# Keeping the split weights of the first attention's projections in DRAM for the second half of the tokens

## The chip, the core and the metric

The kernel runs on one core of a Trainium2 chip. The metric is the time of one execution on the device, in microseconds; three executions of the kernel before took 3351.19 to 3359.43 us, with a median of 3356.41 us. The engines are named as in the profile: PE is TensorE's matmul, PEld its weight load, DVE is VectorE, ACT is ScalarE, POOL is GpSimd, and SP is SyncE, which issues the transfers.

## What is computed

Two blocks are applied to 2048 tokens of 1024 features. The first block is a short convolution mixer and then a stick-breaking attention with 8 heads of 64. The change concerns the four projections of that attention:

```python
kv = _rmsnorm(x, norm_kv) @ w_kv            # w_kv: 1024 x 1024
k, v = jnp.split(kv, 2, axis=-1)
...
h = _rmsnorm(x, norm_b[j])
q, g = jnp.split(h @ w_in_b[j], 2, axis=-1) # w_in_b: 1024 x 1024
...
o = _stick_breaking_attention(q, k, v)
x = x + (o * jax.nn.silu(g)) @ w_out_b[j]
```

The second block has a gated pooling mixer and an attention over the 256 best keys of an indexer (`w_in`, `w_out`). Everything is float32.

## The kernel before

**Precision.** A float32 product is made of three matmuls in the type `fp32r`. Each operand is split into a rounded part `hi` and a remainder `lo`, and `lin` (L112 to L122) adds `hi*hi`, `hi*lo` and `lo*hi` (L119, L120, L121) over the blocks of 128 features. One call of `lin` makes 128 outputs for 512 tokens, with 24 matmuls for 1024 features.

**Stages.** Tokens are handled in two halves of 1024. `phase_a(h)` is the convolution mixer, `phase_b(h)` makes k, v, q and the gate of the attention, `phase_c(h)` is the attention itself, `phase_d` its output projection and the next norm, `phase_e` and `phase_e2` the second block's projections, `phase_f` its attention and `phase_g` the output. `phase_b` first normalises the tokens (`norm_x`, L313 to L320: load from `x1d`, multiply on DVE at L319, round on ACT at L81, subtract on DVE at L82), and then runs through 16 blocks of 128 columns: eight of `w_kv` (four k, four v) and eight of `w_in_b` (four q, four gate). For each block it calls `load_w` once and `lin` twice (512 tokens each), and stores k, q (`hi` and `lo` each), v or the gate to DRAM. `phase_c` loads them again: z is two matmuls (L533, L534), ACT's sigmoid follows (L536), DVE's scan (L546) and multiply (L547), the transposes on PE (L553), ACT's copy (L555) and the matmul with v (L561).

**Weights.** `load_w` makes two tiles for a block of 1024 features, one for each four blocks of features. A tile is loaded raw into one of two buffers (`raw`, shown as `fixed`), for `w_kv` and `w_in_b` multiplied by the norm's gain on DVE (L103), rounded on ACT into the `hi` half of one of four slots (`weights`, shown as `fixedr`; L104), and the remainder is put into the `lo` half by DVE (L105). A slot holds 512 KB, a raw tile 256 KB. With `keep` the slot is also stored to DRAM (L107 to L109, `kept_<name>_<column>_<block>`), and a later call with the same name, column and block loads the slot from there at L95 and skips the rest. Before the change that is so for `w_out`, `w_out_b`, `w_in` and `w_pool`; `w_in_a` and `w_out_a` are called with `keep=False`; `w_kv` and `w_in_b` are left out by name at L106. All transfers are issued by SP (`dma`, L75 to L77), in order, so all show line L77.

**Order.** The phases are generators, merged by weights; `ahead` raises the priority of one of them, and a planner then lays out the instructions of each engine by data dependences, priorities and its own estimate of times. The calls around the change are:

```python
run(self.phase_b(0, xa))                                                    # L1340
merge((self.phase_b(1, xb), 167), (self.ahead(self.phase_c(0), 2000), 95))  # L1342
merge((self.ahead(self.phase_c(1), 2000), 260), (de, 300))                  # L1344
```

So `phase_b(0)` runs alone (about 905 to 1100 us in the profile), `phase_b(1)` runs beside the attention of the first half (about 1100 to 1480 us), and after that the attention of the second half runs beside `phase_d(0)` and `phase_e(0)`.

Of the kernel before, what the change touches and what calls it, by code (L numbers as in the profile page):

```python
# [68 lines left out]
class Build:  # L69
# [14 lines left out]
    def load_w(self, name, nk, c0, m=P, gain=None, after=None, keep=True, own=None):  # L84

        nc = self.nc
        hi, lo = [], []
        for k0 in range(0, nk, 4):
            t = self.turn("weights", 4) if own is None else own
            hi += [t[:, 0, k] for k in range(4)]  # L90
            lo += [t[:, 1, k] for k in range(4)]
            if (name, c0, k0) in self.kept:
                if after is not None:
                    nc.gpsimd.tensor_copy(t[:, :, 0, 0:1], after.unsqueeze(2).to_broadcast([P, 2, 1]))
                self.dma(t, self.kept[name, c0, k0])  # L95
                continue
            raw = self.turn("raw", 2)
            if m < P:
                nc.gpsimd.memset(raw, 0.0)
            self.dma(raw[:, :, :m], self.I[name][k0 * P : (k0 + 4) * P, c0 : c0 + m].rearrange("(k p) m -> p k m", p=P))  # L100
            if gain is not None:
                g = self.vec[:, gain + k0 : gain + k0 + 4]
                nc.vector.tensor_tensor(raw, raw, g.unsqueeze(2).to_broadcast([P, 4, P]), ALU.mult)  # L103
            nc.scalar.activation(t[:, 0], raw, AF.Copy)  # L104
            nc.vector.tensor_tensor(t[:, 1], raw, t[:, 0].bitcast(F32), ALU.subtract)  # L105
            if keep and name not in ("w_kv", "w_in_b"):  # L106
                d = self.dr.tile([P, 2, 4, P], F32R, name=f"kept_{name}_{c0}_{k0}")  # L107
                self.dma(d, t)
                self.kept[name, c0, k0] = d  # L109
        return hi, lo  # L110
# [1369 lines left out]
```

## Time and profile before

| | before |
|---|---|
| median of 3 executions | 3356.41 us |
| lowest, highest | 3351.19, 3359.43 us |
| the profiled execution | 3360.51 us |
| its span, first to last instruction | 3358.8 us |
| mean granted clock of TensorE | 0.977 |
| PE, DVE, ACT busy | 96%, 67%, 45% of the span |

Busy shares are means over stages with different limits, so the stretches of the two calls of `phase_b` are read one by one. A busy PE is not PE at its peak, since the ends of matmuls are modelled and overlap; the starts of matmuls and the busy time of the weight loads say how fast it really goes. The granted clock stands as a share of full speed, between the level 1.2 GHz (0.5) and 2.4 GHz (1.00).

### The profile page before, as it was taken

The page shows a single profiled execution, that of the slowest core. Times are in us where ns is not written, and L with a number is a line of the kernel's source. Part 1 is how long each engine was busy: PE and PEld are TensorE (multiplying, and loading weights), DVE is VectorE, ACT ScalarE, POOL GpSimd, SP SyncE. Part 2 cuts the span into 40 slices and gives each one's busy share as a digit, 9 for nine tenths or more (in the row PEclk, how much of TensorE's full clock was granted, in tenths as well). Part 3 has the DMA queues.
Part 4 walks back from the last instruction along what each step waited for, and adds up shares of the span by engine and source line. Part 5 has one row for each costly group of instructions (what it writes and reads, how often), then busy time and mean ns, then how long its engine had stood idle before and what let it go on. Part 6 is the DMA issues. An engine that isn't in the chain of part 4 may idle for free.

```text
span 3358.8 us, 49679 instructions
## 1 busy us (share of the span) xinstructions
PE 3212.6 (96%) x18050; PEld 2546.6 (76%) x18050; DVE 2249.0 (67%) x4516; ACT 1501.3 (45%) x2794; POOL 470.9 (14%) x584
## 2 busy tenths in 40 slices
PE   8999999999999999998899999889999999999997
PEld 7888888788878778776678887667877777666775
DVE  5344534545253878788888788798946878799741
ACT  4111421111232544465555555565365555776571
POOL 0000010000100000033312112331110143103002
PEclk9999999999999999997999999889999999999998
DMA  3111452424454455474456544554553265115115
GB/s 105 48 48 47 138 169 88 132 85 138 129 179 154 143 153 160 127 245 131 117 157 182 171 141 158 168 168 135 172 164 105 84 214 171 47 39 172 46 30 180
DMA packets 371683, 439.77 MB, mean 131 GB/s; under 512 B 25696, under 2 KB 271968, under 8 KB 371424
## 3 DMA queue, kind: packets, MB, share of 16 engines
q1 hardware_dynamic: 371424, 436.44, 42.1%
q8 instruction: 147, 2.41, 0.3%
q14 instruction: 112, 0.92, 0.1%
HBM read 309.46 MB, written 125.30 MB: 129 GB/s over the span
## 4 chain that ended last, share of the span: by engine, by line
PE 78%; DVE 13%; ACT 3%; issue 3%; DMA 2%; POOL 0%; SPq 0%; ACTq 0%; DVEq 0%; POOLq 0%
PE lin L119 11%; PE lin L120 10%; PE lin L121 10%; PE z L119 4%; PE z L120 4%; PE z L121 4%; PE o L561 4%; PE o L1221 3%; PE tp L553 3%; PE tp L1213 3%; PE tp L120 3%; PE tp L119 3%; PE tp L121 3%; DVE crf L546 2%; PE z L533 2%
## 5 line engine op out<-in xcount | busy, mean ns | idle before, releaser
L119 PE MATMUL lin<-act,fixedr 128*128 128x512 f32 x1488 | 597.4, 402 | 15.0 <-DVE x1r L597 7.9
L120 PE MATMUL lin<-act,fixedr 128*128 128x512 f32 x1488 | 595.2, 400 | 9.5 <-DVE act L618 7.2
L121 PE MATMUL lin<-act,fixedr 128*128 128x512 f32 x1488 | 592.2, 398 | 0.0
L104 ACT ACTIVATE fixedr<-fixed 128x512 fp32r<-128x512 f32 x294 | 185.9, 634 | 726.1 <-PE lin L120 263.2
L546 DVE TENSOR_TENSOR_SCAN crf<-crf 128x512 f32<-128x512 f32 (+3 forms) x320 | 354.6, 1116 | 74.0 <-ACT crf L543 71.4
L119 PEld LDWEIGHTS lin<-act,fixedr 128*128 128x128 f32 x1488 | 284.0, 191 | 80.3 <-DVE x1r L597 9.8
L120 PEld LDWEIGHTS lin<-act,fixedr 128*128 128x128 f32 x1488 | 283.8, 191 | 74.3 <-DVE act L618 10.0
L105 DVE TENSOR_TENSOR fixedr<-fixed,fixedr 128x512 fp32r<-128x512 f32 x294 | 203.5, 693 | 197.7 <-ACT fixedr L104 186.2
L121 PEld LDWEIGHTS lin<-act,fixedr 128*128 128x128 f32 x1488 | 283.7, 191 | 61.0 <-issue 0.2
L1162 DVE CUSTOM_DVE_ANT_0 fe<-z,masks 128x512 f32<-128x512 f32 (+3 forms) x320 | 188.3, 605 | 105.0 <-PE tp L1213 53.3
L119 PE MATMUL z<-act,fixedr 128*128 128x512 f32 x584 | 231.7, 397 | 9.3 <-ACT fixedr L104 9.3
L536 ACT ACTIVATE crf<-z 128x512 f32<-128x512 f32 (+3 forms) x320 | 175.3, 549 | 144.6 <-PE tp L553 109.8
L555 ACT COPY crf<-tp 128x512 f32<-128x512 f32 (+3 forms) x320 | 164.9, 532 | 156.0 <-PE tp L553 135.8
L120 PE MATMUL z<-act,fixedr 128*128 128x512 f32 x584 | 231.0, 396 | 0.0
L121 PE MATMUL z<-act,fixedr 128*128 128x512 f32 x584 | 230.9, 396 | 0.0
L549 POOL TENSOR_TENSOR crf<-crf 128x1 f32<-128x1 f32 x192 | 93.2, 487 | 928.8 <-ACT crf L536 732.5
L1176 ACT ACTIVATE fe<-fe,fixed 128x1024 f32<-128x1024 f32 (+7 forms) x192 | 189.7, 992 | 71.6 <-DVE fixed L1173 70.8
L1215 ACT COPY ff<-tp 128x512 f32<-128x512 f32 (+3 forms) x320 | 161.2, 523 | 127.2 <-PE o L1221 65.7
L883 DVE SCALAR_TENSOR_TENSOR sc<-ff,fixed,sc 128x512 f32<-128x512 f32 (+3 forms) x266 | 180.8, 702 | 52.3 <-ACT ff L876 50.5
L547 DVE TENSOR_TENSOR crf<-crf 128x511 f32<-128x511 f32 (+3 forms) x320 | 199.8, 630 | 10.7 <-PE lin L121 0.5
L1213 PE MATMUL tp<-fixed,fe 128*128 128x128 f32 x1088 | 181.8, 282 | 21.0 <-ACT fe L1176 16.4
L876 ACT ACTIVATE ff<-z 128x512 f32<-128x512 f32 (+3 forms) x304 | 158.2, 547 | 92.2 <-PE z L874 73.1
(346 smaller groups left out, 6541.5 us busy)
## 6 DMA issues: line engine op xcount, KB each, us to landing
fixed<-in_w_in_a_dram SPq DMA_DIRECT2D x128, 256.0 KB, 2.7
fixedr<-kept_w_out SPq DMA_DIRECT2D x64, 512.0 KB, 4.8
kept_w_in<-fixedr SPq DMA_DIRECT2D x46, 512.0 KB, 4.1
fixedr<-kept_w_in SPq DMA_DIRECT2D x46, 512.0 KB, 4.0
crr<-kst SPq DMA_DIRECT2D x80, 256.0 KB, 5.4
crr<-qst SPq DMA_DIRECT2D x64, 256.0 KB, 5.4
fixed<-x2d SPq DMA_DIRECT2D x64, 256.0 KB, 3.8
ffr<-q2s SPq DMA_DIRECT2D x128, 128.0 KB, 2.9
```

The source lines that it names most:

```text
L104: nc.scalar.activation(t[:, 0], raw, AF.Copy)
L105: nc.vector.tensor_tensor(t[:, 1], raw, t[:, 0].bitcast(F32), ALU.subtract)
L119: self.nc.tensor.matmul(ps[:, :n], whi[k], a, start=k == 0, stop=False)
L120: self.nc.tensor.matmul(ps[:, :n], whi[k], b, start=False, stop=False)
L121: self.nc.tensor.matmul(ps[:, :n], wlo[k], a, start=False, stop=k == nk - 1)
L536: nc.scalar.activation(s[:, :W], z[:, :W], AF.Sigmoid)
L546: nc.vector.tensor_tensor_scan(er, er, er, left, ALU.mult, ALU.min)
L547: nc.vector.tensor_tensor(s[:, : W - 1], s[:, : W - 1], e[:, 1:W], ALU.mult)
L883: nc.vector.scalar_tensor_tensor(sc[:, c0 : c0 + m], r[:, :m], w, sc[:, c0 : c0 + m], ALU.mult, ALU.add)
L1162: nc.vector.tensor_tensor_reduce(row[c0 // HT][:, c0 % HT : c0 % HT + m], z[:, :m], mb[:, c0 : c0 + m], 1.0, NEG, ALU.subtract, ALU.max, m ...
L1176: nc.scalar.activation(x, x, AF.Exp, bias=nbs, scale=sc, accum_out=den[:, u, hd : hd + 1])
L1213: nc.tensor.transpose(tp[:, j * P : (j + 1) * P], pe[a][k0 // HT][:, k0 % HT : k0 % HT + P], self.ident)
```

## The change

The exclusion of `w_kv` and `w_in_b` at L106 is dropped:

```diff
-            if keep and name not in ("w_kv", "w_in_b"):
+            if keep:
                 d = self.dr.tile([P, 2, 4, P], F32R, name=f"kept_{name}_{c0}_{k0}")
                 self.dma(d, t)
                 self.kept[name, c0, k0] = d
```

`phase_b(0)` now stores each of its 32 split tiles (16 blocks of columns, two tiles each) to DRAM, with the gain already in them. `phase_b(1)` loads them from there at L95 into the weight slots, without the raw buffer, the multiply of L103, the rounding of L104 and the subtraction of L105.

## Rows read from the trace of the kernel before

**Rows 1.** Head of the page: span, busy time and share by engine.

```profile
span 3358.8 us, 49679 instructions
PE 3212.6 (96%) x18050; PEld 2546.6 (76%) x18050; DVE 2249.0 (67%) x4516; ACT 1501.3 (45%) x2794; POOL 470.9 (14%) x584
```

**Rows 2.** Busy time by stretch: from:to, length, engines in order, clock, DMA, GB/s.

```profile
core 0: us, PE busy (x) PEld busy (x) DVE busy (x) ACT busy (x) POOL busy (x), PEclk, DMA share, GB/s
960.00:1100.00 140.00, 140.00 (x637) 115.82 (x635) 53.17 (x81) 31.67 (x55) 0.00 (x0) 1.00 0.58 175
1100.00:1480.00 380.00, 372.00 (x2297) 294.40 (x2297) 310.10 (x537) 186.63 (x388) 29.56 (x52) 0.99 0.54 161
1120.00:1220.00 100.00, 94.12 (x562) 73.16 (x560) 87.82 (x164) 49.93 (x107) 5.31 (x11) 0.97 0.56 165
1240.00:1340.00 100.00, 99.90 (x652) 80.60 (x651) 82.73 (x155) 43.31 (x97) 4.65 (x10) 1.00 0.56 147
1340.00:1480.00 140.00, 137.99 (x852) 108.47 (x851) 105.48 (x158) 73.91 (x142) 17.89 (x28) 1.00 0.55 180
```

**Rows 3.** PE's waits, 1100 to 1480 us: releaser, us in total, times, longest.

```profile
PE lin L120 <- DVE act L82: 2.3, 1, 2.3
PE z L533 <- DMA crr<-qst: 1.8, 1, 1.8
```

**Rows 4.** Groups by line, 1110 to 1400 us: busy, mean ns, idle before, releaser.

```profile
L104 ACT ACTIVATE fixedr<-fixed 128x512 fp32r<-128x512 f32 x28 | 17.7, 635 | 33.0 <-PE lin L120 30.0 <-DVE fixed L103 3.0
...
L103 DVE TENSOR_TENSOR fixed<-fixed 128x512 f32<-128x512 f32 x29 | 20.0, 690 | 36.2 <-DMA fixed<-in_w_in_b_dram 22.3 <-DMA fixed<-in_w_kv_dram 13.8
L105 DVE TENSOR_TENSOR fixedr<-fixed,fixedr 128x512 fp32r<-128x512 f32 x28 | 19.0, 678 | 0.0
```

**Rows 5.** DVE in order of time, phase_b(1)'s norm: first and last of nine.

```profile
1126.14 0.67 DVE L105 TENSOR_TENSOR fixedr<-fixed,fixedr 128x512 fp32r<-128x512 f32 x1
...
1180.80 0.67 DVE L105 TENSOR_TENSOR fixedr<-fixed,fixedr 128x512 fp32r<-128x512 f32 x1
```

**Rows 6.** Stores: KB each, median us to landing; then landing of kept_w_in's 46 loads.

```profile
kept_w_in<-fixedr SPq DMA_DIRECT2D x45, 512.0 KB, 4.1
...
DMA to landing us min/median/max: 3.1/4.0/8.6
```

**Rows 7.** phase_b(0): ACT and DVE in order of time; DVE's waits, 905 to 960 us.

```profile
1057.61 0.63 ACT L104 ACTIVATE fixedr<-fixed 128x512 fp32r<-128x512 f32 x1 [0.66 <-PE z L120]
1068.49 0.63 ACT L104 ACTIVATE fixedr<-fixed 128x512 fp32r<-128x512 f32 x1 [1.90 <-PE lin L120]
...
1058.89 0.68 DVE L105 TENSOR_TENSOR fixedr<-fixed,fixedr 128x512 fp32r<-128x512 f32 x1
...
1062.20 0.69 DVE L103 TENSOR_TENSOR fixed<-fixed 128x512 f32<-128x512 f32 x1 [0.51 <-DMA fixed<-in_w_in_b_dram]
...
DVE fixed L319 <- DMA fixed<-x1d: 2.7, 6, 1.0
```

**Rows 8.** SP's waits, 1100 to 1480 us; then 2170 to 2620 us.

```profile
SPq L77 <- DVE fixedr L105: 100.1, 26, 11.1
...
SPq L77 <- PE lin L121: 103.0, 29, 14.3
```

**Rows 9.** SP and PE in order of time; then the stretch behind, as rows 2.

```profile
1181.49 8.47 SPq L77 DMA_DIRECT2D fixed<-in_w_kv_dram  x2
1190.06 1.17 SPq L77 DMA_DIRECT2D crr<-qst  x2
...
1197.34 0.30 PE L533 MATMUL z<-crr 128*128 128x128 f32 x1 [1.78 <-DMA crr<-qst]
...
1200.00:1220.00 20.00, 20.00 (x120) 15.62 (x118) 15.71 (x31) 8.20 (x20) 0.58 (x3) 0.94 0.60 181
```

**Rows 10.** PE's waits, 2620 to 3359 us: a kept load that came late.

```profile
PE lin L119 <- DMA fixedr<-kept_w_out: 6.8, 1, 6.8
```

**Rows 11.** Busy time behind the merged stretch, columns as in rows 2.

```profile
1480.00:3359.00 1879.00, 1757.34 (x11021) 1370.86 (x11019) 1445.18 (x3294) 1058.71 (x2012) 393.00 (x454) 0.97 0.44 136
```

## The prediction, made before the changed kernel was run

> **What bounds the kernel now.** I read the head of the page first: TensorE (PE) is busy for 3212.6 of 3358.8 us, so whatever is to shorten the kernel must be a wait of PE or a time in which PE runs slowly [rows 1]. The change touches two calls only: `phase_b(0)`, which computes k, v, q and gate of the first 1024 tokens alone, and `phase_b(1)`, which does the same for the second half while `phase_c(0)`, the attention of the first half, runs beside it. So I read those stretches next [rows 2]. In phase_b(0) after its norm (960 to 1100 us) PE is busy for 140.00 of 140.00 us at granted clock 1.00, while VectorE (DVE) is busy 53.17 us and ScalarE (ACT) 31.67 us. In the merged stretch (1100 to 1480 us) PE is still busy for 372.00 of 380 us, but DVE now for 310.10 us, and 8.0 us of PE are idle. The third thing to see is where these 8.0 us lie: 5.9 us of them are between 1120 and 1220 us, where phase_b(1) normalises its tokens, and the two longest waits of the stretch are for the DVE half of that norm (2.3 us) and for a load of q (1.8 us) [rows 3].
>
> The first row of PE hides something. The weight loads (PEld) are busy for 80.60 us per 100 us where the merged stretch runs without a wait (1240 to 1340 us), for 73.16 us between 1120 and 1220 us and for 108.47 us in the 140 us from 1340 to 1480 us [rows 2]. Taken at 80.6 per 100 us, the work of these two pieces would have needed 90.8 and 134.6 us; they lost 9.2 and 5.4 us, 14.6 us together, where PE's own idle time says 5.9 and 2.0 us. The difference holds the lowered clock (mean 0.97 from 1120 to 1220 us) and gaps too short to show. That is the most which the merged stretch can give back. The Trainium skill ("Perfetto Trace Analysis", section "Identifying the Most-Contended Engine") says that matmul busy time is not a good measure of the distance to the roofline and that the busy share of the weight loads is. By PE's idle time the change could bring 8.0 us at most, by the weight loads 14.6 us, and this trace gives both numbers.
>
> **The change part by part.** *Removed in phase_b(1).* 32 weight tiles (8 column blocks of `w_kv` and 8 of `w_in_b`, two tiles each) lose their gain multiply on DVE (L103, 690 ns), their rounding on ACT (L104, 635 ns) and their subtraction on DVE (L105, 678 ns) [rows 4]. That is 32 x 1.37 = 43.8 us of DVE and 32 x 0.635 = 20.3 us of ACT. DVE's share of the merged stretch falls from 82% to about 70%. Nearly all of it lies beside a busy PE and is worth nothing there. On the path lies what falls into the norm: from 1126 to 1181 us DVE works with hardly a stop, and nine of the removed instructions (the first L105 at 1126.14, the last at 1180.80) stand in that queue [rows 5], each some 0.6 us from start to start (L105 ends 0.68 us after its start, the overlap with the next taken off). That is 5.4 us by which the queue of DVE ends earlier; PE's 2.3 us wait stands in the middle of it. A second part: ACT works in order, and its L104 had to wait for PE to release the weight slot, 30.0 us of idle time, with the sigmoids and copies of the attention queued behind; DVE's L103 waited for raw loads for some 36 us, with the scans queued behind [rows 4]. Both waits go away. PE shows little of them (1240 to 1340 us has 0.1 us idle), so I bound this part by zero and by the rest of the 14.6 us, 9.2 us, and take 1.6 us, near the lower end, since PE had other work in most of these waits. Sum: -7 us.
>
> *Moved in phase_b(1).* The load on SyncE's (SP) queue becomes one of 512 KB into the weight slot in place of one of 256 KB into the raw buffer, and it waits for another thing. Before, SP waited for L105 to release the raw buffer (100.1 us in 26 waits); for the kept weights of `w_in`, later in the kernel, it waits for PE's last read of the slot (103.0 us in 29 waits, the longest 14.3 us) [rows 8]. So SP stands about as long as before. Queued behind it are the loads of q, k and v for the attention, the stores of k, q and gate, and those who wait for them are the z matmuls (L533, L534). The weights themselves arrive in time: the slots of a block are free when the block before the running one is done, and the running block has 48 matmuls beside the attention; a kept load lands in 4.0 us (median) and 8.6 us at most, and for none of the 46 kept loads of `w_in` did an engine wait [rows 6]. The nearest row against it is one PE wait of 6.8 us for a kept load of `w_out` in the last phase [rows 10]. I bound this part by 0 and +6.8 us and take 0, by the 46 loads, which stand in the more similar stage. A gain is excluded here, because the weights were never late before.
>
> *Added in phase_b(0).* 32 stores of 512 KB, each landing in 4.1 us (median of the stores of `w_in`) [rows 6]. SP issues each behind the wait for L105 that the next raw load has anyway. Behind it stand that raw load and the stores of k and q. Room for that: ACT began to fill a slot at 1057.61 us, when PE had left it, and L105 had finished it by 1059.57 us; ACT fills the first slot of the next block at 1068.49 us, 10.9 us later [rows 7], and PE is not idle meanwhile. A store issued at 1059.6 us would read its slot until 1063.7 us, and the slot is written again two blocks later, at some 1079.4 us. The raw load that the store goes ahead of arrives at 1062.20 us (L103) and is needed by L104 at 1068.49 us [rows 7]; after 0.69 us of L103 that leaves 5.6 us, more than a whole store's 4.1 us. DMA: 0.58 busy at 175 GB/s is 302 GB/s at full share; 32 x 0.524 MB over the 195 us of phase_b(0) (905 to 1100 us) are 86 GB/s more, so 261 GB/s or 0.86 of the 16 engines. That is busy, not full; in phase_b(1) 32 x 0.262 MB in 380 us are 22 GB/s more, 0.54 becomes 0.61 [rows 2]. The one place without cover is the norm of phase_b(0), where DVE waited for tokens (`x1d`) for 2.7 us in 6 waits [rows 7]. The stores of the four tiles split before it are issued by about 926 us, before most of these loads, so I take 0 and bound it by +4.1 us, one store ahead of the last token load. A gain is excluded, since PE has no idle time to give from 960 us on.
>
> The sum is made against the profiled execution: 3358.8 us of span, 3360.5 us with what lies around it, 4.1 us above the median of 3356.4 us. 3360.5 - 7 = 3353.5 us there, and 3349 us in terms of the median. A measurement of this kernel can tell 0.3%, some 10 us, from no change, so -7 us counts as within it. What is late next is the norm's own chain (token load, DVE multiply, ACT rounding, DVE subtraction) and then the head of the second attention.
>
> **The rivals.** *Faster (A):* the blocked queues of ACT and DVE, not the norm alone, are what thins PE's work out. For it: the weight loads fall behind from 1340 to 1480 us too, and L104's waits are spread over the whole stretch [rows 2, 4]. Against it: from 1240 to 1340 us the same waits exist and PE lost 0.1 us. It gives back the 14.6 us whole, 3342 us; with the uncertainty of the 80.6 (the single stretch that it is read from) 3335 to 3346 us.
>
> *Slower (B):* SP's queue. A kept load is issued in SP's order, and while it waits for PE to leave a slot, the q and k loads of the attention behind it wait too. The trace has one such case now: SP stood for 8.47 us at two raw loads, the q load went out at 1190.06 us, and PE idled 1.78 us for it before 1197.34 us [rows 9]; the clock behind it (mean 0.94 over the next 20 us) costs 0.06 x 20 = 1.2 us more. phase_c(0) loads q in eight groups. If all eight are hit it is 8 x 3.0 = 24 us, 3380 us; if half, 12 us, 3368 us; it decides from some four groups on. For it: the wait is for PE, which is the slowest to release anything, and phase_c stands ahead of phase_b in priority. Against it: in the second half's projections SP waits in the same way as long in total [rows 8] and no row there names a kept load as late.
>
> *Reordered (C):* the planner lays out the queues anew, and the later phases are mixed otherwise. From 1480 us on PE lacks 1879 - 1757 = 122 us [rows 11]; a tenth of that in either direction is 12 us, 3344 to 3368 us. *It does not do what it says:* the key (name, column, k block) is the same for both halves and the tile already has its gain, so the second half does find its weights; I give this no chance of its own.
>
> **How the numbers follow.** Forecast (-2 to -10 us, 3346 to 3354 us): 0.42. A: 0.32. B: 0.17. C: 0.09, a third each to faster, same, slower. Faster by over 0.3%: 0.32 + 0.03 = 0.35. Within: 0.42 + 0.03 = 0.45. Slower: 0.17 + 0.03 = 0.20. The likeliest time is 3349 us. The range reaches from A's farther end to B with half the groups hit, 3333 to 3369 us; outside stay B's worse half (0.08), the tail of A (0.05) and those of C (0.04).
>
> **What would show it.** Right: L103 at 32 instructions, L104 and L105 at 32 fewer; the DVE queue of phase_b(1)'s norm ends some 5 us earlier and the wait for L82 shrinks; no PE wait names a load of `kept_w_kv` or `kept_w_in_b`; phase_b(0) has PE busy at 100% after its norm with a DMA share near 0.86. A: PEld near 80 per 100 us over the whole merged stretch. B: waits of the z matmuls for q or k loads with SP waiting for PE ahead of them. Wrong: PE waits in phase_b(0), or a change of more than 10 us behind 1480 us.

## The result and the profile after

The changed kernel takes 3340.35 us (median of 7 executions, 3338.53 to 3342.52), the kernel before 3359.43 us in the same comparison (7 executions, 3351.19 to 3367.78). The ratio is 0.995, with a 95% interval of 0.9935 to 0.9964: 0.5% faster, 19 us. My forecast was 3349 us and "no change that can be told"; the time lies within the range that I gave, on the side that I held to be second in likelihood.

The same lines of the page and of the views, now of the changed kernel. First the head of the page (compare [rows 1]):

```profile
span 3338.6 us, 49602 instructions
PE 3201.1 (96%) x18050; PEld 2539.2 (76%) x18050; DVE 2207.8 (66%) x4452; ACT 1483.3 (44%) x2762; POOL 453.0 (14%) x584
```

The span is 20.2 us shorter. DVE lost 64 instructions and 41.2 us, ACT 32 and 18.0 us, as the change says. PE is busy for 11.5 us less with the same 18050 matmuls, and idle for 137.5 us instead of 146.2. Then the busy times by stretch (compare [rows 2]; the last line answers to [rows 11]):

```profile
960.00:1100.00 140.00, 139.53 (x631) 115.17 (x630) 51.10 (x78) 31.86 (x54) 0.00 (x0) 1.00 0.81 271
1100.00:1480.00 380.00, 373.49 (x2321) 294.60 (x2319) 280.49 (x484) 171.16 (x364) 21.99 (x52) 1.00 0.60 181
1120.00:1220.00 100.00, 95.31 (x577) 73.72 (x576) 82.20 (x151) 47.62 (x105) 5.21 (x12) 0.98 0.67 195
1240.00:1340.00 100.00, 98.83 (x642) 79.10 (x641) 71.67 (x137) 38.89 (x89) 1.89 (x9) 1.00 0.60 170
1340.00:1480.00 140.00, 139.36 (x867) 109.84 (x865) 98.17 (x142) 69.93 (x138) 13.36 (x28) 1.00 0.58 185
...
1480.00:3339.00 1859.00, 1746.39 (x11009) 1365.60 (x11009) 1436.27 (x3286) 1056.98 (x2008) 382.25 (x453) 0.97 0.44 138
```

In the merged stretch DVE's share fell from 82% to 74% (280.49 of 380 us), and PE's weight loads are busy for 294.60 us where they were for 294.40: by this view the stretch whose queues the change relieves gained next to nothing. The view is not quite fair, since a weight load of L119 takes 188 ns at the full clock and 330 ns at the lowered one (medians, kernel before), and the clock was lowered a little less here after the change. 24 matmuls more start in the stretch, some 4 us at 380/2297 us each (an estimate, since matmuls differ in length), so a few us at most are gained here. The larger part of the gain lies behind 1480 us. That can be followed through three lines that run once for each group or column block, the last step of an attention group (L576), of `phase_d` (L597) and of a projection of `phase_e2` (L785). Their duration, then their first and last start, before and after:

```profile
L576 DVE TENSOR_TENSOR crf<-o,crf x16: 678/684/692, 1132.3 to 2135.2; 128x512 f32<-128x512 f32 x16
...
L597 DVE TENSOR_TENSOR x1r<-lin,x1r x32: 636/682/693, 1447.8 to 2215.5; 128x512 f32<-128x512 f32 x32
...
L785 DVE TENSOR_TENSOR fixed<-lin,fixed x32: 660/685/693, 1865.4 to 2629.3; 128x512 f32<-128x512 f32 x32
```

```profile
L576 DVE TENSOR_TENSOR crf<-o,crf x16: 678/684/693, 1133.7 to 2125.2; 128x512 f32<-128x512 f32 x16
...
L597 DVE TENSOR_TENSOR x1r<-lin,x1r x32: 664/682/693, 1460.4 to 2202.4; 128x512 f32<-128x512 f32 x32
...
L785 DVE TENSOR_TENSOR fixed<-lin,fixed x32: 664/686/693, 1863.9 to 2613.1; 128x512 f32<-128x512 f32 x32
```

The first attention group ends 1.4 us later than before, the second attention 10.0 us earlier, `phase_d(1)` 13.1 us, `phase_e2` 16.2 us, the kernel 20.2 us. Between the first group and the last the lead does not grow evenly. Here are the last group of the first attention and the first one of the second, before and after:

```profile
L576 DVE TENSOR_TENSOR crf<-o,crf x2: 684/688/692, 1415.0 to 1498.2; 128x512 f32<-128x512 f32 x2
```

```profile
L576 DVE TENSOR_TENSOR crf<-o,crf x2: 678/684/690, 1411.5 to 1487.7; 128x512 f32<-128x512 f32 x2
```

The attention was 3.5 us ahead at the one and 10.5 us at the other, while PE as a whole had gained a few us at most: the attention had moved ahead of the projections. So the steps to look at are the second attention, beside `phase_d(0)` and `phase_e(0)` from 1480 us on, and what follows it from 2100 us on. PE's waits from 1480 to 1700 us, before (releaser, us in total, times, longest):

```profile
PE tp L553 <- DVE crf L547: 9.7, 7, 4.9
PE lin L119 <- DVE x1r L597: 5.1, 3, 2.4
PE lin L726 <- POOL fixed L725: 4.8, 2, 4.3
```

and after:

```profile
PE tp L553 <- ACT crf L555: 5.6, 1, 5.6
PE lin L120 <- DVE act L618: 4.6, 5, 2.0
PE tp L553 <- DVE crf L547: 4.4, 6, 2.0
PE lin L119 <- DVE x1r L597: 3.8, 3, 1.6
```

The transposes of the attention wait 5.3 us less for DVE's multiply (L547), and the wait for POOL's L725, which belongs to `phase_e(0)`, is gone; but a wait of the transposes for ACT's copy (L555) came in with 5.6 us, and the one for L618 grew. All of PE's waits there come to 28.9 us before and 27.0 us after, so the difference is small. The granted clock is the second part, here of two stretches, before and after:

```profile
1480.00:1700.00 220.00, 190.76 (x1214) 147.76 (x1213) 186.68 (x253) 120.42 (x231) 74.13 (x79) 0.90 0.50 146
2100.00:2300.00 200.00, 170.16 (x948) 128.77 (x946) 173.01 (x441) 121.64 (x260) 65.21 (x58) 0.90 0.55 163
```

```profile
1480.00:1700.00 220.00, 193.55 (x1256) 151.70 (x1257) 193.14 (x255) 126.68 (x242) 74.27 (x83) 0.92 0.53 156
2100.00:2300.00 200.00, 173.21 (x977) 132.45 (x975) 173.84 (x498) 124.40 (x269) 67.84 (x66) 0.91 0.53 165
```

PE starts 42 matmuls more in the first of these and 29 more in the second. None of this is what my sum was made of, so the experiments ask two things: how much of the 19 us belongs to the change at all, and which part of the change it belongs to.

### The profile page after: what moved, and what is told of

It reads as the page before. It is cut to its first block, busy times and chain, and to the rows that moved or that the text cites. A ratio compares the mean times of both kernels' runs of the same rounds, so it can differ in the third digit from the quotient of the medians.

```text
span 3338.6 us, 49602 instructions
## 1 busy us (share of the span) xinstructions
PE 3201.1 (96%) x18050; PEld 2539.2 (76%) x18050; DVE 2207.8 (66%) x4452; ACT 1483.3 (44%) x2762; POOL 453.0 (14%) x584
## 5 line engine op out<-in xcount | busy, mean ns | idle before, releaser
L119 PE MATMUL lin<-act,fixedr 128*128 128x512 f32 x1488 | 594.0, 400 | 15.1 <-DVE x1r L597 5.6
L104 ACT ACTIVATE fixedr<-fixed 128x512 fp32r<-128x512 f32 x262 | 165.7, 633 | 680.3 <-PE tp L120 221.1
L119 PEld LDWEIGHTS lin<-act,fixedr 128*128 128x128 f32 x1488 | 282.5, 190 | 79.4 <-DVE x1r L597 7.3
L105 DVE TENSOR_TENSOR fixedr<-fixed,fixedr 128x512 fp32r<-128x512 f32 x262 | 181.5, 693 | 172.9 <-ACT fixedr L104 167.2
L119 PE MATMUL z<-act,fixedr 128*128 128x512 f32 x584 | 232.1, 398 | 10.5 <-ACT fixedr L104 10.5
L555 ACT COPY crf<-tp 128x512 f32<-128x512 f32 (+3 forms) x320 | 165.1, 531 | 156.4 <-PE tp L553 136.0
L549 POOL TENSOR_TENSOR crf<-crf 128x1 f32<-128x1 f32 x192 | 86.5, 452 | 933.8 <-ACT crf L536 804.8
L547 DVE TENSOR_TENSOR crf<-crf 128x511 f32<-128x511 f32 (+3 forms) x320 | 200.2, 631 | 11.2 <-PE o L121 0.5
L1213 PE MATMUL tp<-fixed,fe 128*128 128x128 f32 x1088 | 181.7, 283 | 17.5 <-ACT fe L1176 14.0
```

The costliest lines, as they stand in the source:

```text
L119: self.nc.tensor.matmul(ps[:, :n], whi[k], a, start=k == 0, stop=False)
L547: nc.vector.tensor_tensor(s[:, : W - 1], s[:, : W - 1], e[:, 1:W], ALU.mult)
L1213: nc.tensor.transpose(tp[:, j * P : (j + 1) * P], pe[a][k0 // HT][:, k0 % HT : k0 % HT + P], self.ident)
```

## The experiments

Each time below is a median; the ratio, with its 95% interval, is to the kernel before in the same comparison (medians 3358.73, 3359.01 and 3359.36 us on the three chips used) and is not exactly the quotient of the two medians. "adaln weight" is the 9 in `merge((self.phase_a(1, xa, xb), 420), (self.adaln(), 9))`, a merge that stands ahead of `phase_b`. Another number there changes nothing of the work, but makes the planner lay out the queues anew.

**How much is the order's luck.** Two runs in a second order, the kernel before and the changed one:

```diff
-            merge((self.phase_a(1, xa, xb), 420), (self.adaln(), 9))
+            merge((self.phase_a(1, xa, xb), 420), (self.adaln(), 10))
```

> The kernel before, with one number of the merge changed (the weight of adaln beside phase_a(1), 9 to 10): the same work, laid out by the planner in another order. Theory R (relief: the 43.8 us taken off DVE let the attention run ahead of the second half's projections, so that phase_c(1) ends some 10 us earlier and phase_d(1) begins earlier): within 5 us of before, 3354 to 3364 us, the end of phase_c(1) (last L576) near 2135 us. Theory O (order: the gain of 19 us is one of two layouts that differ by luck): it may land anywhere within some 20 us of before, and 3340 us would be no surprise.

> The changed kernel with the same number changed (9 to 10). Theory R: 15 to 20 us below e1_before_order2, near 3340 us, the last L576 10 us earlier than in e1_before_order2. Theory O: its distance to e1_before_order2 has no set sign; it may well be 0 or the other way.

Measured: before in this order 3359.39 us, ratio 1.001 [1.000, 1.002]; the change 3350.62 us, 0.9974 [0.9964, 0.9984]. Two more with the weight 8, a third order:

> The kernel before in a third order (weight of adaln 9 to 8). Theory R (relief of the queue ahead of the attention): within 5 us of before, 3354 to 3364 us, last L576 within 3 us of 2135 us. Theory O (luck of the order): anywhere within 20 us of it.

> The changed kernel in the third order. Theory R: last L576 some 10 us earlier than in e5_before_order3, and the time 8 to 19 us below it; the 8 is what e2_change_order2 gained on e1_before_order2, the 19 what the change itself gained on before, and the part beyond some 9 us is luck of the order behind phase_c(1). Theory O: no set sign.

Measured: before 3363.17 us, 1.0013 [1.0001, 1.0024]; the change 3352.72 us, 0.9977 [0.9964, 0.9990]. So the change is worth 19.1, 8.8 and 10.5 us in three orders. It is faster in each, and about half of what its own order shows is that order's luck. Neither expectation had this: theory R asked for 15 to 20 us in the second order, theory O for no set sign. The stretch from 1480 to 1700 us in the second order and then in the third, each before and after, shows the same as in the change's own order, more matmuls at a higher clock:

```profile
1480.00:1700.00 220.00, 189.44 (x1230) 147.04 (x1231) 190.66 (x258) 123.87 (x237) 71.94 (x82) 0.91 0.49 146
1480.00:1700.00 220.00, 193.25 (x1249) 150.53 (x1249) 191.49 (x252) 125.29 (x238) 70.70 (x82) 0.92 0.53 152
...
1480.00:1700.00 220.00, 189.65 (x1202) 147.82 (x1200) 188.50 (x255) 121.26 (x232) 72.77 (x80) 0.88 0.49 144
1480.00:1700.00 220.00, 191.57 (x1232) 149.88 (x1233) 193.29 (x253) 124.42 (x236) 70.51 (x82) 0.91 0.54 153
```

In the merged stretch the weight loads change by 1.5 and -0.9 us in these two orders, with 31 and 16 matmuls more.

**The stores and the loads.** One run makes no stores; its second half loads tiles that `w_out` has kept (same size, same slot), so that k, v, q and gate of the second half are computed from other weights (an edit of the kernel before):

```diff
+            if name in ("w_kv", "w_in_b"):
+                n = self.split_once.setdefault((name, c0, k0), len(self.split_once))
+                if (name, c0, k0) in self.second:
+                    src = self.kept["w_out", n // 2 % 8 * P, 4 * (n % 2)]
+                    self.dma(t, src)
+                    continue
+                self.second.add((name, c0, k0))
...
+        self.split_once, self.second = {}, set()
```

> e2_change_order2 without the 32 stores: phase_b(1) loads the tiles kept for w_out in place of its own weights (so k, v, q and gate of the second half are made with other weights and without the gain), phase_b(0) stores nothing. The phases after it do the same work. Theory R: as e2_change_order2 or up to 3 us faster, since phase_b(0) got 3.0 us longer with the stores. If the stores cost more than phase_b(0) shows: faster by more than 5 us.

The other makes the stores, and its second half splits the raw weights as before:

```diff
                 self.dma(d, t)
-                self.kept[name, c0, k0] = d
+                if name not in ("w_kv", "w_in_b"):
+                    self.kept[name, c0, k0] = d
```

> The second order (adaln weight 10): the 32 stores are made in the first half, the second half splits the raw weights again as before. It is to be set against the second order of the kernel before (3359.4 us) and of the change (3350.6 us). My step for the stores was 0 with a bound of 4.1 us; the runs with and without stores differ by some 3 us at the first attention's start. Theory 1 (stores cost time in phase_b(0) through the DMA share of 0.81, and nothing later makes up for it): first L576 some 3 us later and the total 3361 to 3364 us. Theory 2 (the delay is absorbed where PE has waits): first L576 3 us later, total 3358 to 3361 us. Theory 3 (the stores, not the loads, make the gain): 3350 us.

Both are in the second order. Loads alone: 3351.54 us, 0.9976 [0.9967, 0.9985], the time of the whole change there. Stores alone: 3361.36 us, 1.0012 [0.9998, 1.0025], 2.0 us above the kernel before in that order. In this order the loads carry the gain; the stores cost nothing that can be told, 2.0 us by one pair and -0.9 us by the other (3350.62 - 3351.54).

**DVE's time.** The first attempt put the 32 pairs of DVE instructions back, each behind a kept load in the program, on stale data in the raw buffer, so that they wait for nothing:

```diff
                 self.dma(t, self.kept[name, c0, k0])
+                if name in ("w_kv", "w_in_b"):
+                    raw = self.turn("raw", 2)
+                    g = self.vec[:, gain + k0 : gain + k0 + 4]
+                    nc.vector.tensor_tensor(raw, raw, g.unsqueeze(2).to_broadcast([P, 4, P]), ALU.mult)
+                    nc.vector.tensor_tensor(raw, raw, raw, ALU.subtract)
```

> e2_change_order2 with the DVE time put back: behind each kept load of phase_b(1) DVE multiplies the idle raw buffer by the gain and subtracts it from itself, 2 x 32 instructions of the removed shapes that wait for nothing and that nobody waits for. ACT's rounding stays out, and so do the waits for raw loads and for the slots. Theory R, if it is DVE's time: the gain is gone, within 5 us of e1_before_order2, last L576 as late as there. If it is the waits of DVE and ACT in order, not their time: it stays within 5 us of e2_change_order2. Theory O: anywhere.

Measured: 3392.05 us, 1.0095 [1.0077, 1.0114], 41 us above the change in the same order (3350.62 us). The planner put all 32 pairs into the norm, between 1080 and 1200 us, since nothing held them back (groups of this kernel there, then busy times of 1100 to 1200 us):

```profile
L100 DVE TENSOR_TENSOR fixed<-fixed 128x512 f32<-128x512 f32 x32 | 21.7, 683 | 0.0
L99 DVE TENSOR_TENSOR fixed<-fixed 128x512 f32<-128x512 f32 x32 | 21.6, 686 | 0.1
...
1100.00:1200.00 100.00, 89.31 (x460) 68.08 (x459) 98.85 (x180) 38.19 (x80) 8.56 (x8) 0.95 0.53 164
```

DVE is nearly full there (98.85 of 100 us), and 43.3 us of it cost 41 us. So this run says what DVE's time is worth where it is crowded, and not what the removed instructions were worth in their places. For that, each pair has to stand behind its own load:

```diff
+                if name in ("w_kv", "w_in_b"):
+                    raw = self.turn("raw", 2)
+                    g = self.vec[:, gain + k0 : gain + k0 + 4]
+                    nc.vector.tensor_tensor(raw, t[:, 0].bitcast(F32), g.unsqueeze(2).to_broadcast([P, 4, P]), ALU.mult)
+                    nc.vector.tensor_tensor(raw, raw, t[:, 1].bitcast(F32), ALU.subtract)
```

(behind the kept load; nobody reads the result). It ran in the third order and in the change's own:

> e6_change_order3 with the DVE time put back where it was: behind each kept load DVE multiplies the loaded hi half by the gain into the raw buffer and subtracts the lo half from it, 2 x 32 instructions of the removed shapes, each of which waits for its load as L103 waited for the raw load; nobody uses the result. ACT's rounding and its wait for the slot stay out. If DVE's time and place in the queue are the cause: the gain is gone, last L576 within 3 us of e5_before_order3 and the time within 5 us of it. If ACT's blocked queue is the cause: as e6_change_order3. Half and half: in the middle.

> The changed kernel in its own order (adaln weight 9, as in the kernel before), with one more pair of DVE instructions behind each kept load of the second half (gain multiply of the loaded high part into the raw buffer, subtraction of the loaded low part; results unused), so DVE's 43.8 us stand in the merged stretch again, each pair behind its own load. Theory 1 (the loaded weights themselves matter, not DVE's time: nothing of the weights stands in ACT's queue and no raw load is waited for): the lead of the first attention goes, as in the third order, but PE's waits between 1480 and 1700 us stay short and the time stays near the changed kernel's, 3338 to 3347 us. Theory 2 (DVE's time is the gain): most of the 19 us goes, 3352 to 3360 us. Theory 3 (about half of the 19 us is what this order of the later phases happens to be worth): the layout changes once more and the time lies near the third order's 3346 us or higher, up to 3353 us, with the gain up to the end of the second attention (last L576) still 9 us or more.

Measured: 3345.67 us, 0.9954 [0.9938, 0.9970], 7.0 us below the change in the third order; and 3349.83 us, 0.9973 [0.9959, 0.9987], 9.5 us above the change in its own. The merged stretch of the third-order run and one of its DVE groups there:

```profile
1100.00:1480.00 380.00, 371.73 (x2285) 294.56 (x2285) 310.04 (x540) 168.27 (x356) 29.34 (x52) 0.99 0.60 182
...
L99 DVE TENSOR_TENSOR fixed<-fixedr,fixed 128x512 f32<-128x512 f32 x32 | 22.0, 689 | 32.2 <-DMA fixedr<-kept_w_in_b 18.6 <-DMA fixedr<-kept_w_kv 13.5
```

DVE is busy for 310.04 us, as in the kernel before (310.10 us, [rows 2]), and again stands waiting for a load of the weights; the mean of the two effects is +1.2 us. The 43.8 us of DVE are worth nothing that these runs can tell from the order's scatter, which is as large as either effect. What they do show is that the gain stands without the freed DVE time: with it put back the kernel is 17.5 and 9.5 us below the kernel before in the same order. The lead of the attention does not stand: the first group of the second attention starts its L576 at 1499.9 and 1503.9 us in these two runs, at 1498.7 and 1498.2 us in the kernel before in the same orders. So DVE's time gave the attention its lead, and the gain stands without that lead. The times fit none of the expectations wholly: none had a run below the change, and the second run lies in theory 3's range, but its last L576 starts at 2134.9 us, where that theory had 9 us or more ahead of the 2135.2 us before.

**ACT's time as well.** The same, with a copy on ACT between the two, in the third order:

```diff
                     nc.vector.tensor_tensor(raw, t[:, 0].bitcast(F32), g.unsqueeze(2).to_broadcast([P, 4, P]), ALU.mult)
+                    nc.scalar.activation(raw, raw, AF.Copy)
                     nc.vector.tensor_tensor(raw, raw, t[:, 1].bitcast(F32), ALU.subtract)
```

> e7_dve_paced with ACT's time back too: between the two DVE instructions ACT copies the raw buffer (635 ns, 32 times), but without the wait for PE that L104 had. If DVE alone is the cause: as e7_dve_paced within 5 us. If ACT's time counts: later than e7_dve_paced by up to 20 us. If only ACT's wait for the slot counts: as e7_dve_paced, and both as e6_change_order3.

Measured: 3355.81 us, 0.9983 [0.9973, 0.9994], 10.1 us above the run without the copy and 3.1 us above the change in this order. In the merged stretch the weight loads are busy for 290.82 us instead of 294.56, so there it does cost PE some 5 us (3.74 / 0.806, the busy share at a full PE from [rows 2]):

```profile
1100.00:1480.00 380.00, 368.68 (x2254) 290.82 (x2254) 305.55 (x533) 182.40 (x382) 21.31 (x48) 0.99 0.58 178
...
L100 ACT ACTIVATE fixed<-fixed 128x512 f32<-128x512 f32 x32 | 20.4, 638 | 51.7 <-DVE fixed L99 51.6
```

ACT stands for 51.6 us at these copies, and the sigmoids queue behind. By the expectation ACT's time counts; but against the change the difference is within the scatter of orders. Still, with all the engine work of the split back in the second half and only its result not needed, the kernel is 7.4 us faster than the one before in this order.

**One removed instruction at a time.** Two runs without kept weights, in which the second half leaves out one of the three steps, so that its slot keeps an older part and k, v, q and gate of the second half are computed from that. (The weight of a late merge, 250, is 242 in both.) The rounding on ACT, L104:

```diff
+            again = name in ("w_kv", "w_in_b") and (name, c0, k0) in self.halves_seen
+            self.halves_seen[name, c0, k0] = True
...
-            nc.scalar.activation(t[:, 0], raw, AF.Copy)
+            if not again:
+                nc.scalar.activation(t[:, 0], raw, AF.Copy)
...
+        self.halves_seen = {}
```

> Nothing stored or loaded split for these two matrices, as before, but the second half leaves the rounding on ACT (L104) out: the slot keeps an older high part, so k, v, q and gate of the second half are wrong, and nothing else is skipped. ACT loses 32 x 0.635 = 20.3 us and the slot wait passes from ACT to the subtraction on DVE. The weight of one later merge is 242 in place of 250, which lays out the end of the kernel anew. Theory 1 (ACT's queue, in which the rounding stood behind the slot, is the cause of the gain around 1560 to 1700 us): the second attention's last L576 starts 9 us or more ahead of before, total 3340 to 3352 us. Theory 2 (raw loads and DVE's time count): DVE now holds the slot wait itself, the lead of the first attention is gone, last L576 within 4 us of before, total 3355 to 3365 us. Theory 3 (only the layout): anything within 10 us of 3359 us, with no PE wait changed in kind.

and the subtraction on DVE, L105, left out in the same way:

> As the kernel before, but the second half leaves the subtraction on DVE (L105) out: the slot keeps an older low part, so k, v, q and gate of the second half are wrong. DVE loses 32 x 0.678 = 21.7 us, of which some 5 instructions stood in the norm. ACT's rounding with its slot wait stays. Same other weight as the run with no rounding. Theory 1 (ACT's queue): the first attention runs ahead by a few us (c(0) end -2), but PE's waits at 1480 to 1700 us stay as before, and the last L576 is within 4 us of before; total 3354 to 3362 us. Theory 2 (DVE's time): about half of what the change gave up to the last L576, -5 us, total 3348 to 3356 us.

Measured: 3355.64 us, 0.9999 [0.9985, 1.0012], and 3357.33 us, 0.9997 [0.9983, 1.0011]. Neither alone is a gain that can be told. The kernel before was not measured with the weight 242, so a few us of order are in both, and a small part for either step is not excluded: from 1480 to 1700 us PE starts 1254 and 1263 matmuls in these runs, as the kernels do that load split (1232 to 1312), and not as the four do that split wholly (1202 to 1232). Each count is of one profiled execution, and the one without the subtraction was 7.6 us faster than the mean of its kernel.

**All runs in one table.** Of every execution the span and the mean granted clock are known. "Lost to the clock" is (1 - clock) x span, the mean over all executions of a kernel, and "rest" is span minus that. From the profiled execution of each stand two more numbers: the first and last start of the norm's subtraction (L82) in `phase_b(1)`, and the sum of PE's waits for L547 (the attention's multiply) and for POOL's L725 between 1480 and 1700 us (the lines as numbered in the kernel before).

| kernel | executions | span | lost to the clock | rest | L82 | waits L547 + L725 |
|---|---|---|---|---|---|---|
| before | 35 | 3357.3 | 72.9 | 3284.4 | 1132.9 to 1165.6 | 9.7 + 4.8 |
| before, second order | 11 | 3359.9 | 80.6 | 3279.3 | 1133.4 to 1166.2 | 9.2 + 3.8 |
| before, third order | 12 | 3362.1 | 81.8 | 3280.3 | 1134.0 to 1166.9 | 10.6 + 2.9 |
| stores only, second order | 12 | 3360.6 | 73.1 | 3287.5 | 1135.8 to 1170.4 | 12.7 + 2.9 |
| no rounding | 12 | 3355.1 | 71.3 | 3283.8 | 1136.1 to 1169.7 | 5.6 + 4.1 |
| no subtraction | 12 | 3355.0 | 71.3 | 3283.7 | 1132.5 to 1168.0 | 7.6 + 3.5 |
| change | 7 | 3338.4 | 62.5 | 3276.0 | 1134.3 to 1171.8 | 4.4 + 0 |
| change, second order | 11 | 3350.0 | 66.7 | 3283.3 | 1134.5 to 1172.1 | 4.4 + 0.9 |
| change, third order | 12 | 3350.7 | 70.1 | 3280.6 | 1134.0 to 1171.9 | 7.3 + 0.8 |
| loads only, second order | 11 | 3349.7 | 67.6 | 3282.1 | 1131.6 to 1168.4 | 4.9 + 1.0 |
| DVE paced, own order | 12 | 3347.5 | 67.8 | 3279.7 | 1138.1 to 1172.5 | 4.7 + 2.8 |
| DVE paced, third order | 6 | 3343.6 | 62.4 | 3281.2 | 1135.0 to 1170.4 | 4.9 + 0.5 |
| DVE and ACT paced, third order | 12 | 3354.1 | 65.7 | 3288.4 | 1137.2 to 1170.5 | 2.2 + 2.3 |

The first six rows split the weights from raw tiles in the second half, two of them with a step left out; the last seven load them split, three of them with work put back. The mean span is 3358.3 and 3347.7 us, 10.6 us apart, and the two sets don't overlap in span (their nearest rows are 0.9 us apart), in the time lost to the clock (71.3 to 81.8 against 62.4 to 70.1, means 75.2 and 66.1) or in the last column (9.7 us and more against 8.1 us and less). The rest overlaps wholly (3283.2 and 3281.6 in the mean). Pair by pair, in the three orders, the change takes 18.9, 9.9 and 11.4 us off the mean span and 10.4, 13.9 and 11.7 us off the time lost to the clock. The run with all DVE pairs in the norm, which loads split too, is left out of the table; its span is 3390.4 us, its time lost to the clock 83.1 us.

The last column holds only the two waits that fell. The new wait for ACT's copy (L555) stands with 5.6 to 5.9 us in all three orders of the change, and all of PE's waits from 1480 to 1700 us come to 28.9, 30.0 and 30.0 us in the kernel before and to 27.0, 26.3 and 29.0 us in the change. So PE does not wait much less there; it waits for something else.

So where the gain shows: of the 10.6 us by which the two sets differ in the mean, some 9 us stand in the time lost to the clock. 9 us lost to the clock are 18 us at 1.2 in place of 2.4 GHz. In the profiled executions of the kernel before and the change, the start of the second attention holds most of it: summed over windows of 20 us, the time lost to the clock is 22.4 us before and 17.4 us after from 1480 to 1700 us, and 3.6 and 1.6 us from 1100 to 1480 us. This is an account and not a cause. The sum counts a lowered clock also where PE stands waiting, and a lowered clock can itself come from a wait of PE: in [rows 9] it followed one of 1.78 us, with 0.94 over the next 20 us. The change's own order has another 8.4 us in the rest (3284.4 - 3276.0), which the second and third order don't have (-4.0 and -0.3 us): the order's luck. The split of a span into these two parts itself moves by 8 us from one order to the next (72.9 and 80.6 for the kernel before), so I hold the 10.6 us for firmer than its parts.

What stays open is why the second attention begins with a higher clock and more matmuls when the weights come split, when `phase_b(1)` is over. It doesn't need the freed time of DVE, and it isn't the stores. In the runs with the work put back the gain stands as long as the weights themselves don't wait for DVE and ACT; that this is what makes it is not shown. Whether it works through the raw buffers, through the slot's wait in ACT's queue, or through the order that the planner makes of other due times, none of these runs tells apart.

## Why the prediction was right or wrong

*The instruction counts*: right. L103, L104 and L105 over the whole run, after, where before had 64, 294 and 294:

```profile
L105 DVE TENSOR_TENSOR fixedr<-fixed,fixedr 128x512 fp32r<-128x512 f32 x262 | 181.5, 693 | 172.9 <-ACT fixedr L104 167.2 <-ACT crf L536 3.4 <-PE z L121 1.2
L104 ACT ACTIVATE fixedr<-fixed 128x512 fp32r<-128x512 f32 x262 | 165.7, 633 | 680.3 <-PE tp L120 221.1 <-PE lin L120 218.1 <-PE z L120 114.4
L103 DVE TENSOR_TENSOR fixed<-fixed 128x512 f32<-128x512 f32 x32 | 22.1, 690 | 56.6 <-DMA fixed<-in_w_in_b_dram 40.5 <-DMA fixed<-in_w_kv_dram 16.0
```

*5.4 us from the norm's queue on DVE*: this is the step that failed, and with it the sum. I let each removed instruction pull the rest of DVE's queue forward by its own length [rows 5]. The instructions did go: DVE is busy for 82.20 us from 1120 to 1220 us, 5.6 us less than before. But the norm's last L82 starts at 1171.8 us instead of 1165.6. The norm takes 37.5 us from its first to its last L82 where it took 32.7, and 36.8 us or more in all four runs of the change and of the loads alone. The planner did not keep the order and close the gaps; it laid the queue out anew, and the norm's steps came to stand further apart. PE's weight loads in that stretch rose from 73.16 to 73.72 us, 0.7 us of full work, where the sum had 5.4 us. PE's wait for L82 did shrink (from 2.3 to 0.9 us, [rows 3]), and another took its place; PE's waits from 1100 to 1480 us, after:

```profile
PE lin L119 <- DVE bl L409: 1.5, 1, 1.5
PE z L533 <- DMA crr<-qst: 1.2, 1, 1.2
PE tp L553 <- DVE crf L547: 1.1, 3, 0.4
PE lin L120 <- DVE act L82: 0.9, 2, 0.6
```

*1.6 us from the blocked queues, and rival A's 14.6 us*: wrong in size and in place. By A the weight loads should have risen to 80 per 100 us over the whole stretch; they are at 79.10 from 1240 to 1340 us and 109.84 in 140 us from 1340 us on, where 0.806 x 140 = 112.8 were needed. A's time, 3342 us, comes close to the measured one by accident, the mechanism didn't happen. The 14.6 us were also read from a doubtful measure: they take the busy time of the weight loads for work, but with the clock lowered, as for a part of the stretch from 1120 to 1220 us, one weight load of L119 is busy for 330 ns in place of 188. Where DVE's freed time went is shown by its scan, from 1200 to 1400 us, before and after:

```profile
L546 DVE TENSOR_TENSOR_SCAN crf<-crf 128x512 f32<-128x512 f32 (+3 forms) x67 | 65.0, 978 | 1.7 <-ACT crf L543 0.8
```

```profile
L546 DVE TENSOR_TENSOR_SCAN crf<-crf 128x512 f32<-128x512 f32 (+3 forms) x66 | 64.8, 989 | 20.4 <-ACT crf L543 19.3
```

DVE now stands idle for 19.3 us ahead of the scans, waiting for ACT's L543; the number of scans is nearly the same (67 and 66). PE is busy for 99.90 and 98.83 of 100 us from 1240 to 1340 us, before and after, so a less busy DVE mostly waits.

*The stores at 0, bound 4.1 us*: right, 2.0 and -0.9 us in the two pairs. The DMA share of `phase_b(0)` was 0.81 at 271 GB/s from 960 to 1100 us, where I had worked out 0.86 at 261 GB/s; PE is busy for 139.53 of 140 us.

*The loads at 0, and rival B*: right, and B is out. No PE wait of the merged stretch names `kept_w_kv` or `kept_w_in_b` as its releaser. SP waits for PE to leave the slots as I had forecast from the later phases (103.0 us there, [rows 8]), and the z matmuls wait for q no longer than before in this stretch (1.2 us after, 1.8 before, [rows 3]); one wait of 3.0 us for q came in behind it, between 1650 and 1700 us. SP's waits from 1100 to 1480 us, after:

```profile
SPq L77 <- PE lin L121: 97.0, 21, 12.7
...
SPq L77 <- DVE fixedr L105: 18.4, 3, 10.2
```

*A change of more than 10 us behind 1480 us*: I had named this as what would show the prediction wrong, and it came. Rival C had the place and, with 12 us, the size, but I gave it 0.09 in all and a third of that to "faster". The runs show two things in it that I took for one: a scatter of the order, which is 4 us among three orders of the kernel before and 12 us among three of the change, and a gain that all seven kernels with split loads in the table show in their mean span. I had read the 122 us which PE lacks behind 1480 us [rows 11] as noise for the planner, and left out the clock that goes with them.

So the time was in the range and "faster" the second likeliest of my three cases, but the sum of -7 us was right in neither of the two terms that it is made of, and that the range held was luck as far as the mechanism goes. The norm's queue ended later and not earlier, the merged stretch gave a few us at most, and most of the 9 to 19 us shows in stretches whose instructions the change does not touch.

## What to carry to other kernels

Where a planner lays out the queues, a removed instruction doesn't pull its queue forward by its own length: ask what PE was waiting for there, and where it was busy for nearly all of the stretch, as here (372.00 of 380 us), expect little in that stretch. Price such a change in neighbouring orders too, with two or three harmless changes of the layout before and after: here 19 us in one order were 9 and 10 in two others. And put removed work back behind the same wait that it had; put back without one, it was moved into the one crowded place and cost 41 us, where behind its own loads it cost nothing that could be told.

## What the runs showed of the chip that I had not expected

The kernel before takes between 3347.21 and 3368.41 us in 35 executions on one chip, while its mean span is nearly the same on three chips (3357.4, 3357.9 and 3357.3 us). In most kernels a good part of the scatter goes with the mean granted clock of the execution: the correlation between span and clock is -0.66 over these 35 executions and -0.90 over the 11 of the run with loads only, but -0.14 over the 7 of the change and 0.36 over the 6 of the run with DVE paced in the third order. A single profile can therefore be some 8 us off its kernel: the profiled execution of the run without the subtraction had a clock of 0.982 and a span of 3347.4 us, where the mean of its 12 executions is 0.979 and 3355.0 us.
